# Second block's output projection: the groups' row scale ahead of the split, all partial sums in PSUM banks

## Chip, core and metric

One Trainium2 chip, one of its cores. The metric is the device time of one launch in microseconds (us); the kernel before is stated by the median of three runs.

## What is computed

Two blocks run one after the other on 256 tokens of width 1024, each two layers deep: a first block (latent attention, a gated recurrence, a gated feed-forward part) and a second block, a hybrid of windowed attention and a state-space mixer, with a gated feed-forward part. All inputs are float32. The part that matters is the end of the second block's mixer (`attn` has 512 columns, `y` 1024 in two groups of 512):

```
y = ssd_chunked(xs, dt, a_neg, bm, cm) + d_skip[:, None] * xs
y = y.reshape(bsz, s, SSM_INNER) * silu(z)
y = rmsnorm(y.reshape(bsz, s, 2, 512), ssm_norm.reshape(2, 512))     # a mean of squares per token and group
return concatenate([attn, y.reshape(bsz, s, 1024)], axis=-1) @ w_out   # 1536 x 1024, added to the residual x
```

Behind it comes `h = h + swiglu(rmsnorm(h))`, which needs the whole sum.

## The kernel before

Activations lie feature-major: a tile has 128 features on the partitions and the 256 tokens on the free axis; the residual stream `x` is eight such chunks. Products of float32 are made of three matmuls in fp32r (`mm3`, L434 to L436): each operand is split into a high and a low half, and high x high, high x low and low x high are accumulated in PSUM. Weights come by DMA in units of 128 x 1024 (`wf`), ScalarE copies the high half (`wh`, L409), VectorE subtracts to get the low half (`wl`, L410). There are three `wf` buffers and six each of `wh` and `wl`, used in turn, so the copy of a unit waits until TensorE is done with the unit six before it.

`layer_b` (L1021) is one layer of the second block. Its end: the gate `z` is multiplied out (L1255) and passed through silu; per pair p of chunks (0 to 3; group 0 is pairs 0 and 1, group 1 pairs 2 and 3) the state-space output is finished by matmuls (L1236, L1242) and VectorE's `dskip` step (L1238), product (L1244) and add (L1245). Then `out_residual` makes the attention part of the output projection: for each of four pairs of output chunks one unit of weights, 2 x 4 x 3 matmuls into a fresh PSUM bank (tag `mm`, four banks), and an add of the bank to `x` (L571). Each group is gated (L1264), squared (L1266), its squares added (L1273, L1275); its rows, scaled by the norm's gain alone, are split into high and low halves (L482, L483; tile `r`). `token_rsqrt` sums the squares over the partitions with a small matmul (L500), scales the mean (L502) and takes the power -1/2 on GpSimd (L503). `bcast_rows` spreads the result over the partitions: a diagonal tile `dg` (L489), a matmul with ones (L491), ScalarE's copy to `rb` (L493). `out_residual` runs again for each group on the unscaled rows: the bank is multiplied by `rb` on VectorE (L569), and added to `x` by GpSimd (L571), pair 3 of group 1 by VectorE. `ffn` follows: `norm_prep` splits `x` into `xs` (L482, L483), and `lin_wide` (L455, L456) multiplies.

Within an engine instructions run in one row; which row that is, a scheduler decides when the kernel is built, from its own plan of the engines, so instructions of several stages are interleaved.

## Time and profile before

| | us |
|---|---|
| median of three runs | 1431.85 (1431.1 to 1432.63) |
| the profiled execution | 1431.08 |
| its span, first to last instruction | 1429.3 |
| TensorE busy | 1410.8 |
| VectorE busy | 1125.7 |
| ScalarE busy | 853.9 |
| GpSimd busy | 137.0 |
| TensorE's mean granted clock | 0.995 |

The profiled execution is one run; its span leaves out 1.8 us around the first and last instruction. A busy TensorE is modelled from starts, since matmuls overlap: two matmuls of 256 columns start 0.12 us apart though each has a duration of 0.28. What counts is therefore where one starts against the one before it. In a timeline row a start, a duration, the engine, the source line and operation, the tiles (out<-in) and a count are followed in brackets by the idle time ahead of it and by what ended that.

### The profile page before, as it was taken

How to read it: one execution, taken by the hardware profiler on the slowest of the kernel's cores; microseconds unless marked ns; L12 is line 12 of the kernel's file. 1: busy time of each engine (PE TensorE's matmuls, PEld its weight loads, DVE VectorE, ACT ScalarE, POOL GpSimd, SP SyncE). 2: the span in 40 equal slices, each digit the busy share in tenths (PEclk: the TensorE clock that was granted, in tenths of full speed). 3: DMA queues.
4: the chain of work that ended last, by engine and by line, in shares of the span. 5: the costliest groups of instructions: out<-in, count | busy, mean ns of one | idle time of the engine just before them, and what ended most of it. 6: DMA issues, size and time to landing. Idle time of an engine off the chain costs nothing.

```text
span 1429.3 us, 25414 instructions
## 1 busy us (share of the span) xinstructions
PE 1410.8 (99%) x9668; PEld 1257.0 (88%) x9668; DVE 1125.7 (79%) x1907; ACT 853.9 (60%) x1517; POOL 137.0 (10%) x167
## 2 busy tenths in 40 slices
PE   9999999999999999999999998999999999999997
PEld 8888988888898889888888998988888998988886
DVE  7897778776678968887766989888766899988754
ACT  7666456654486655666546764566544784666543
POOL 4610000000033000000002010200000200400000
PEclk9999999999999999999999999999999999999999
DMA  7643556555565345556466653465556663465553
GB/s 246 200 145 122 177 163 199 193 166 181 183 208 176 119 133 178 177 193 199 146 195 214 193 178 105 155 196 181 166 185 195 194 192 113 146 202 190 176 174 106
DMA packets 86234, 248.64 MB, mean 174 GB/s; under 512 B 8992, under 2 KB 28768, under 8 KB 86112
## 3 DMA queue, kind: packets, MB, share of 16 engines
q1 hardware_dynamic: 85392, 246.11, 54.0%
q8 instruction: 76, 1.25, 0.3%
q10 hardware_dynamic: 720, 0.91, 0.2%
q14 instruction: 46, 0.38, 0.1%
HBM read 245.87 MB, written 1.11 MB: 173 GB/s over the span
## 4 chain that ended last, share of the span: by engine, by line
PE 76%; issue 14%; DVE 5%; DMA 2%; ACT 2%; POOL 1%; ACTq 0%; POOLq 0%; DVEq 0%
PE mm L455 26%; PE mm L456 13%; PE mm L435 7%; PE mm L434 7%; PE mm L436 7%; PE at L455 5%; PE at L456 3%; DVE wl L410 2%; DMA wf<-in_wa 2%; ACT wh L409 1%; PE at L606 1%; PE at L643 1%; PE at L632 1%; PE rc L900 1%; PE rc L606 0%
## 5 line engine op out<-in xcount | busy, mean ns | idle before, releaser
L410 DVE TENSOR_TENSOR wl<-wf,wh 128x1024 fp32r<-128x1024 f32 (+3 forms) x501 | 560.9, 1126 | 154.1 <-ACT wh L409 148.2
L409 ACT ACTIVATE wh<-wf 128x1024 fp32r<-128x1024 f32 (+3 forms) x501 | 485.2, 972 | 307.3 <-PE mm L455 110.6
L455 PE MATMUL mm<-xs,wh 128*128 128x512 f32 x1344 | 472.5, 394 | 0.0
L456 PE MATMUL mm<-xs,wl 128*128 128x256 f32 x1344 | 377.2, 282 | 0.0
L455 PEld LDWEIGHTS mm<-xs,wh 128*128 128x128 f32 x1344 | 251.3, 187 | 55.5 <-ACT q L778 0.4
L456 PEld LDWEIGHTS mm<-xs,wl 128*128 128x128 f32 x1344 | 253.6, 189 | 1.7 <-issue 0.2
L455 PE MATMUL at<-xs,wh 128*128 128x512 f32 x448 | 157.1, 392 | 0.0
L455 PE MATMUL mm<-h,wh 128*128 128x512 f32 x384 | 135.7, 395 | 0.5 <-DVE x L587 0.5
L456 PE MATMUL at<-xs,wl 128*128 128x256 f32 x448 | 125.2, 280 | 0.0
L456 PE MATMUL mm<-h,wl 128*128 128x256 f32 x384 | 107.0, 279 | 0.0
L503 POOL TENSOR_TENSOR ry<-ry,mhalf 128x2 f32<-128x2 f32 x13 | 13.5, 1038 | 960.1 <-DVE ry L502 881.5
L455 PEld LDWEIGHTS at<-xs,wh 128*128 128x128 f32 x448 | 83.9, 187 | 18.6
L435 PE MATMUL mm<-xs,wh 128*128 128x256 f32 x320 | 91.9, 287 | 0.0
L436 PE MATMUL mm<-xs,wl 128*128 128x256 f32 x320 | 91.3, 285 | 0.0
L434 PE MATMUL mm<-xs,wh 128*128 128x256 f32 x320 | 91.2, 285 | 0.0
L455 PE MATMUL mm<-t,wh 128*128 128x512 f32 x256 | 90.6, 394 | 0.0
L455 PEld LDWEIGHTS mm<-h,wh 128*128 128x128 f32 x384 | 72.0, 188 | 17.8 <-PE mm L456 1.1
L456 PEld LDWEIGHTS at<-xs,wl 128*128 128x128 f32 x448 | 84.5, 189 | 0.2
L672 ACT ACTIVATE pr<-mm 128x256 f32<-128x256 f32 x120 | 44.5, 375 | 61.1 <-PE mm L456 61.1
L587 DVE TENSOR_TENSOR x<-x,mm 128x256 f32<-128x256 f32 x96 | 39.1, 416 | 51.2 <-PE mm L456 51.1
L434 PE MATMUL mm<-r,wh 128*128 128x256 f32 x256 | 74.3, 293 | 4.7 <-DVE x L571 3.4
L435 PE MATMUL mm<-r,wh 128*128 128x256 f32 x256 | 74.9, 294 | 0.0
(339 smaller groups left out, 2713.1 us busy)
## 6 DMA issues: line engine op xcount, KB each, us to landing
wf<-in_fa SPq DMA_DIRECT2D x120, 512.0 KB, 4.0
wf<-in_fb SPq DMA_DIRECT2D x120, 512.0 KB, 4.0
wf<-in_wa SPq DMA_DIRECT2D x100, 512.0 KB, 4.1
wf<-in_wb SPq DMA_DIRECT2D x72, 512.0 KB, 3.9
wf<-in_fa SPq DMA_DIRECT2D x32, 192.0 KB, 2.4
wf<-in_fb SPq DMA_DIRECT2D x32, 192.0 KB, 2.4
r<-ad SPq DMA_DIRECT2D x16, 256.0 KB, 5.9
wf<-in_wa SPq DMA_DIRECT2D x8, 384.0 KB, 3.7
```

The costliest lines, as they stand in the source:

```text
L409: S.activation(wh[:, :c], f, AF.Copy)
L410: (G if self.i in self.pool else V).tensor_tensor(out=wl[:, :c], in0=f, in1=wh[:, :c].bitcast(F32), op=ALU.subtract)
L434: PE.matmul(ps, lhsT=sh, rhs=mh, start=start, stop=False)
L435: PE.matmul(ps, lhsT=sh, rhs=ml, start=False, stop=False)
L436: PE.matmul(ps, lhsT=sl, rhs=mh, start=False, stop=stop)
L455: PE.matmul(wide, lhsT=wh[:, j, c0:c0 + P], rhs=xs[k], start=k == 0, stop=False)
L456: PE.matmul(wide[:, 1], lhsT=wl[:, j, c0:c0 + P], rhs=xs[k][:, 0], start=False, stop=k == tot - 1)
L587: V.tensor_tensor(out=x[:, c], in0=x[:, c], in1=bank[:, o:o + T], op=ALU.add)
L606: PE.matmul(ps[:, h], lhsT=q, rhs=k[:, 0:n * P], start=True, stop=True)
L632: PE.transpose(pt[:, i], probs[u].rearrange("p h (a k) -> p (h a) k", k=P)[:, i], ident)
L643: PE.matmul(po[64 * j:64 * j + 64, i], lhsT=vs(a, 2 * c + j), rhs=PTs[2 * c + j][a], start=a == 0, stop=a == n - 1)
L672: S.activation(gu[:, m], bank[:, T:2 * T], AF.Copy)
```

## The change

The attention part and both groups go into the same accumulators: four banks `mm`, one for each pair of output chunks, except that the second chunk of pair 3 has a bank of its own with the tag `at`. No product is added to `x` in between; after group 1 each pair's bank is added once (pair 3 chunk by chunk). For that the row scale of a group can no longer be applied to the product: `scaled` computes the group's scale, multiplies rows by gain and scale on VectorE (`scalar_tensor_tensor`, eight a layer), and then splits them, in instructions of 512 columns. `gated` does gate, squares and sums earlier in the text. GpSimd has no residual add left, and the multiplications by `rb` are gone.

```diff
-    def lin_fm(ps, units, c0, xh, xl):
+    def lin_fm(ps, units, c0, xh, xl, first=True, last=True):
...
-                mm3(ps, wh[:, j, c0:c0 + P], wl[:, j, c0:c0 + P], xh[k], xl[k], k == 0, k == tot - 1)
+                mm3(ps, wh[:, j, c0:c0 + P], wl[:, j, c0:c0 + P], xh[k], xl[k],
+                    first and k == 0, last and k == tot - 1)
...
+        squares = []
+
+        def gated(g):
+            sq = []
+            for p in (2 * g, 2 * g + 1):
+                V.tensor_tensor(out=conv[p], in0=conv[p], in1=sz[g][:, p % 2], op=ALU.mult)
+                sq.append(sb("m", [P, 2, T]))
+                S.activation(sq[-1], conv[p], AF.Square)
+            V.tensor_tensor(out=sq[0], in0=sq[0], in1=sq[1], op=ALU.add)
+            a = sq[0][:, 0]
+            V.tensor_tensor(out=a, in0=a, in1=sq[0][:, 1], op=ALU.add)
+            squares.append(a)
+
+        def scaled(g):
+
+            rg = bcast_rows(token_rsqrt(squares[g], 1.0 / 512, EPS2), "rc")
+            yh, yl = [], []
+            for p in (2 * g, 2 * g + 1):
+                y = conv[p]
+                h2 = sb("r", [P, 2, T], F32R)
+                l2 = sb("r", [P, 2, T], F32R)
+                for m in range(2):
+                    V.scalar_tensor_tensor(out=y[:, m], in0=y[:, m], scalar=fm(f"ssmn{l}", 2 * p + m), in1=rg,
+                                           op0=ALU.mult, op1=ALU.mult)
+                split(h2, l2, y)
+                yh += [h2[:, m] for m in range(2)]
+                yl += [l2[:, m] for m in range(2)]
+            return yh, yl
...
+            if p == 1:
+                gated(0)
...
-        out_residual(st, mh, ml)
-        ys = []
-        for g in range(2):
...
-                    split(h2[:, m], l2[:, m], y[:, m], fm(f"ssmn{l}", 2 * p + m))
...
-            ys.append((yh, yl, bcast_rows(token_rsqrt(a, 1.0 / 512, EPS2), "at")))
-        for g in range(2):
-            out_residual(st, *ys[g], PA[g])
+        acc = [psm() for _ in range(4)]
+        acc_pair = [b.rearrange("p (m t) -> p m t", m=2) for b in acc]
+        acc = [b[:, m * T:m * T + T] for b in acc[:3] for m in range(2)] + [acc[3][:, 0:T], psq("at")[:, 0:T]]
+        for i in range(3):
+            hs, ls = scaled(i - 1) if i else (mh, ml)
+            for p in range(4):
+                u = st.next()
+                for m in range(2):
+                    c = 2 * p + m
+                    lin_fm(acc[c], u, m * P, hs, ls, i == 0 and (m == 0 or p == 3), i == 2 and (m == 1 or p == 3))
+                    if i == 2 and p == 3:
+                        V.tensor_tensor(out=x[:, c], in0=x[:, c], in1=acc[c], op=ALU.add)
+                if i == 2 and p < 3:
+                    ps = acc_pair[p]
+                    V.tensor_tensor(out=x[:, 2 * p:2 * p + 2], in0=x[:, 2 * p:2 * p + 2], in1=ps, op=ALU.add)
+            if i == 0:
+                gated(1)
```

How the engines' rows change is shown at three places of the first of the two layers; the second layer has the same there. In the changed kernel the line numbers of `mm3` are L433 to L435, those of the weight halves L408 and L409, of gate, add of squares and last add L1234, L1237 and L1239, of the scaling L1251.

TensorE, where the attention part ends (halves `sg` and `q`) and group 0 begins (halves `r`), before:

```order
L435 MATMUL mm_1743_9877<-q_1575_8784,wh_1740_9858 128x256
L436 MATMUL mm_1743_9877<-sg_1574_8783,wl_1741_9859 128x256
L434 MATMUL mm_1769_9963<-r_1745_9894,wh_1767_9958 128x256
L434 MATMUL mm_1774_9997<-r_1745_9894,wh_1772_9992 128x256
L434 MATMUL mm_1779_10031<-r_1745_9894,wh_1777_10026 128x256
L435 MATMUL mm_1769_9963<-r_1746_9895,wh_1767_9958 128x256
```

and changed:

```order
L434 MATMUL at_1733_9773<-q_1575_8784,wh_1744_9865 128x256
L435 MATMUL at_1733_9773<-sg_1574_8783,wl_1745_9866 128x256
L500 MATMUL rc_1748_9902<-ones_81,m_1713_9636 128x1 x2
L491 MATMUL rc_1751_9911<-dg_1750_9908,ones_81 128x256
L500 MATMUL rc_1769_10047<-ones_81,m_1746_9895 128x1 x2
L433 MATMUL mm_1729_9769<-r_1753_9915,wh_1758_9928 128x256
L433 MATMUL mm_1730_9770<-r_1753_9915,wh_1761_9958 128x256
```

The norms' small matmuls (group 0's L500 and L491, group 1's L500) now stand between the attention part and group 0; before they stood 60 and more matmuls further on, among the groups' own.

VectorE at the same place, changed (tile `m` holds the squares, `t` the rows, `dg` the diagonal, `rb` the spread scale):

```order
L409 TENSOR_TENSOR wl_1780_10074<-wf_1778_10072,wh_1779_10073 128x1024
L1239 TENSOR_TENSOR m_1713_9636<-m_1713_9636 128x256
L1225 TENSOR_TENSOR t_1643_9159<-t_1643_9159,hv_1696_9504 128x2x128
L1234 TENSOR_TENSOR t_1643_9159<-t_1643_9159,q_1698_9508 128x512
L409 TENSOR_TENSOR wl_1783_10105<-wf_1781_10103,wh_1782_10104 128x1024
L1234 TENSOR_TENSOR t_1643_9159<-t_1643_9159,q_1698_9508 128x512
L502 TENSOR_SCALAR ry_1749_9905<-rc_1748_9902 128x2
L1237 TENSOR_TENSOR m_1746_9895<-m_1746_9895,m_1747_9898 128x512
L489 TENSOR_SCALAR dg_1750_9908<-cst_78,ry_1749_9905 128x128 x2
L1239 TENSOR_TENSOR m_1746_9895<-m_1746_9895 128x256
L1251 SCALAR_TENSOR_TENSOR t_1611_8947<-t_1611_8947,pfm_76,rb_1752_9913 128x256 x4
L502 TENSOR_SCALAR ry_1770_10050<-rc_1769_10047 128x2
```

Between group 0's last add of squares (L1239) and its scaled mean (L502) stand two gates and a weight split; before, splits of the unscaled rows stood there, and the residual adds of the attention part ahead of them.

ScalarE around the end of group 0, before:

```order
L409 ACTIVATE wh_1819_10280<-wf_1818_10279 128x1024
L493 ACTIVATE rb_1754_9922<-at_1753_9920 128x256
L409 ACTIVATE wh_1822_10286<-wf_1821_10285 128x1024
L493 ACTIVATE rb_1765_9955<-at_1764_9953 128x256
L409 ACTIVATE wh_1830_10338<-wf_1829_10337 128x1024
```

and changed:

```order
L408 ACTIVATE wh_1785_10135<-wf_1784_10134 128x1024
L408 ACTIVATE wh_1788_10166<-wf_1787_10165 128x1024
L408 ACTIVATE wh_1799_10240<-wf_1798_10239 128x1024
L408 ACTIVATE wh_1802_10246<-wf_1801_10245 128x1024
L493 ACTIVATE rb_1773_10058<-rc_1772_10056 128x256
L482 ACTIVATE r_1774_10060<-t_1643_9159 128x512
L482 ACTIVATE r_1776_10066<-t_1643_9159 128x512
```

Group 1's spread scale and the splits of its rows now stand behind four weight copies, the last of which (`wh_1802`) takes the buffer of `wh_1767`, which group 0's last matmuls read.

## Rows read from the trace of the kernel before

**Rows 1.** The page, part 1: busy us (share of the span) xinstructions.

```profile
PE 1410.8 (99%) x9668; PEld 1257.0 (88%) x9668; DVE 1125.7 (79%) x1907; ACT 853.9 (60%) x1517; POOL 137.0 (10%) x167
```

**Rows 2.** Waits of TensorE in the whole span: us in total, times, longest us.

```profile
PE mm L434 <- DVE x L571: 3.4, 2, 1.7
PE rc L500 <- DVE m L1275: 1.6, 1, 1.6
PE mm L434 <- DVE ry L502: 1.2, 1, 1.2
```

**Rows 3.** Timeline of TensorE, first layer of the second block: start us, us.

```profile
871.47 0.28 PE L436 MATMUL mm<-sg,wl 128*128 128x256 f32 x1
...
875.60 0.28 PE L436 MATMUL mm<-sg,wl 128*128 128x256 f32 x1
875.72 0.28 PE L434 MATMUL mm<-r,wh 128*128 128x256 f32 x1
...
877.79 0.39 PE L434 MATMUL mm<-r,wh 128*128 128x256 f32 x1 [1.68 <-DVE x L571]
...
892.41 0.55 PE L434 MATMUL mm<-r,wh 128*128 128x256 f32 x1 [1.22 <-DVE ry L502]
...
908.52 0.40 PE L455 MATMUL mm<-xs,wh 128*128 128x512 f32 x1
```

**Rows 4.** Timeline of TensorE, second layer of the second block.

```profile
1206.47 0.40 PE L434 MATMUL mm<-r,wh 128*128 128x256 f32 x2
1208.55 0.38 PE L434 MATMUL mm<-r,wh 128*128 128x256 f32 x1 [1.68 <-DVE x L571]
...
1219.86 0.59 PE L491 MATMUL at<-dg,ones 128*128 128x256 f32 x2
...
1220.40 0.50 PE L500 MATMUL rc<-ones,m 128*128 128x1 f32 x4
...
1235.28 0.40 PE L455 MATMUL mm<-xs,wh 128*128 128x512 f32 x1
```

**Rows 5.** Windows: us, busy of PE, PEld, DVE, ACT, POOL; PEclk, DMA, GB/s.

```profile
891.62:898.45 6.83, 6.04 (x28) 6.07 (x29) 6.10 (x10) 1.06 (x1) 5.61 (x5) 0.50 0.45 144
1209.06:1212.48 3.42, 3.42 (x17) 3.42 (x18) 3.42 (x8) 0.00 (x0) 0.00 (x0) 0.50 0.11 43
```

**Rows 6.** Groups by line, GpSimd, 875.72 to 908.52: busy, mean ns | idle, releasers.

```profile
L571 POOL TENSOR_TENSOR x<-x,m 128x512 f32<-128x512 f32 (+1 forms) x8 | 10.3, 1300 | 10.5 <-DVE m L569 5.7 <-DVE ry L502 4.8
```

**Rows 7.** Timeline of VectorE, first layer.

```profile
868.05 1.66 DVE L1238 SCALAR_TENSOR_TENSOR t<-t,pfm,rc 128x256 f32<-128x256 f32 x4 [0.20 <-PE rc L1236]
...
871.03 1.22 DVE L410 TENSOR_TENSOR wl<-wf,wh 128x1024 fp32r<-128x1024 f32 x1
872.16 0.42 DVE L1244 TENSOR_TENSOR hv<-at,h 128x256 f32<-128x256 f32 x1
872.50 0.68 DVE L1264 TENSOR_TENSOR t<-t,q 128x512 f32<-128x512 f32 x1
...
877.66 0.87 DVE L483 SCALAR_TENSOR_TENSOR r<-t,pfm,r 128x256 fp32r<-128x256 f32 x2
```

**Rows 8.** Timeline of VectorE, a norm's scaled mean and diagonal, first and second layer.

```profile
885.66 0.16 DVE L502 TENSOR_SCALAR ry<-rc 128x2 f32<-128x2 f32 x1 [0.62 <-PE rc L500]
...
887.58 0.48 DVE L489 TENSOR_SCALAR dg<-cst,ry 128x128 f32<-128x128 f32 x2 [0.23 <-POOL ry L503]
...
1216.51 0.15 DVE L502 TENSOR_SCALAR ry<-rc 128x2 f32<-128x2 f32 x1
...
1217.93 0.48 DVE L489 TENSOR_SCALAR dg<-cst,ry 128x128 f32<-128x128 f32 x2 [0.60 <-POOL ry L503]
```

**Rows 9.** Timeline of ScalarE, first and second layer.

```profile
871.72 1.06 ACT L409 ACTIVATE wh<-wf 128x1024 fp32r<-128x1024 f32 x1 [0.98 <-PE mm L435]
...
873.21 0.63 ACT L1266 ACTIVATE m<-t 128x512 f32<-128x512 f32 x1 [0.43 <-DVE t L1264]
...
1220.49 0.39 ACT L493 ACTIVATE rb<-at 128x256 f32<-128x256 f32 x1 [1.29 <-PE at L491]
```

32 lines of the change are left out of this document (removed).

## The prediction

> **What bounds the kernel now.** I read the page's busy times first: TensorE is busy 99% of the span [rows 1], and the change leaves its count of matmuls as it is. So the time can move only by TensorE's idle time or its clock. The second view is the list of what TensorE waited for [rows 2]: 3.4 us in two waits for a residual add (L571: a PSUM bank that had not been emptied), 1.6 us for the sum of squares (L1275) and 1.2 us for the scaled mean (L502). All lie in the stage that the change rewrites.
>
> The third view is TensorE's own timeline of that stage. In the first of the two layers of the second block the attention part's last matmul starts at 875.60, the first matmul of the state-space groups at 875.72, and the feed-forward part at 908.52 [rows 3]: 32.80 us. In the second layer it is 1206.47 to 1235.28 [rows 4], 28.81 us. The groups' own work is 2 x 96 matmuls at 0.12 us a start (875.60 to 875.72 [rows 3]), 2 x 11.52 = 23.04 us. The rest is the waits above, the small matmuls of the two norms, and the clock: it was granted at 0.50 for 6.83 us and for 3.42 us there [rows 5]. So 9.8 and 5.8 us a layer is all that can be won.
>
> **The change, part by part.** Terms that hide. Per layer GpSimd loses its eight residual adds, 10.3 us [rows 6]; VectorE loses ten multiplications and, on balance, two adds and gains eight scalings; ScalarE's and VectorE's splits get half as many instructions, twice as wide. TensorE's matmuls cover all of that where nothing waits for it: 0. If the cover were gone it would be VectorE's net 3 us a layer, a gain. The wait for a PSUM bank (1.7 us a layer) goes, since the accumulators stay in their banks. The weights keep their order and their DMAs.
>
> The term that costs. Before, the groups were multiplied unscaled and the row scale was applied to the result, so the first matmul of group 0 needed nothing of the norm. Now the scale goes into the operand. In TensorE's new order the sum of squares of group 0, its broadcast, the sum of squares of group 1 and only then the first matmul of group 0 stand in a row, with no other matmul between. TensorE runs its row in order, so it idles until the whole chain is through. I follow the chain from 868.05, where VectorE takes up the `dskip` steps after waiting for TensorE's L1236 [rows 7]; up to there the two kernels have the same instructions, and from there VectorE has no gap.
>
> VectorE, first layer. When one instruction follows another at once it starts 0.08 before the row's end: 1.13 for a weight split (871.03 to 872.16), 0.34 for 256 columns (872.16 to 872.50), so 0.60 for 512 columns, 0.40 for each scaling step [rows 7]. Four `dskip` steps from 868.05 to 869.63; two adds 870.30; tile `hv` 870.64; gate 871.24; `hv` 871.58; gate 872.18; weight split 873.32; two `dskip` steps 874.11; add of squares 874.71; two `dskip` steps 875.50; add 875.84; weight split 876.98; last add of group 0's squares, 0.42, ends at 877.40. TensorE has been idle since 875.72.
>
> From there the chain has two strands. VectorE's own row goes on to 877.66 (add), 878.26 (gate), 879.40 (weight split), 880.00 (gate, ending at 880.08), and only then the scaled mean (L502) starts, at 880.00, although its matmul (0.50 [rows 4]) was through near 878.0. From its start to the diagonal tile's (L489), with GpSimd's power between, the trace has 1.92 and 1.42 us [rows 8]: 881.42 to 881.92. The other strand, ScalarE's square of the last pair (0.63 [rows 9]) and the add behind it, ends earlier, at 881.37. Diagonal 0.48 [rows 8], so 881.90 to 882.40; a handover between engines is 0.03 (872.50 + 0.68 to 873.21 [rows 7, 9]). The broadcast matmul to ScalarE's copy takes 0.63 (1219.86 to 1220.49 [rows 4, 9]), the copy 0.39 [rows 9], two scalings 0.87 (the row at 877.66 [rows 7]), ScalarE's split of 512 columns about 0.63 by the square of that width. Sum from the diagonal's end with handovers: 0.03 + 0.63 + 0.39 + 0.03 + 0.87 + 0.03 + 0.63 + 0.03 = 2.64. The first matmul of group 0 starts at 884.5 to 885.0; I take 884.8, **9.1 us** after 875.72.
>
> Group 1 has a second wait. Its mean and diagonal are early, but the broadcast matmul stands behind group 0's last matmul (start E), and on ScalarE the copy of the broadcast stands behind a weight copy (`wh`) that needs the buffer which that last matmul reads. A weight copy starts 0.25 after such a matmul (871.47 to 871.72 [rows 3, 9]) and takes 1.06, so E + 1.31; VectorE's weight split, which stands ahead of the scalings, E + 2.48; two scalings E + 3.35; split and two handovers E + 4.04. The next matmul would have started at E + 0.12: **3.9 us** idle. Behind the waiting instructions stand the feed-forward part's weights on both engines; they have the 11.5 us of group 1 to catch up, so that costs 0.
>
> Sum at full clock, a layer: 9.1 + 11.52 + 3.92 + 11.52 = 36.06 us against 32.80 and 28.81: +3.3 and +7.2, together **+10.5 us**. The old stage's waits and half-clock stretches are inside the times subtracted.
>
> The clock. After the stall that ended at 892.41 TensorE was at 0.50 until 898.45 [rows 3, 5]; after the one that ended at 1208.55, for 3.42 us until 1212.48 [rows 4, 5]; the first layer's stall that ended at 877.79 [rows 3] drew nothing. At 0.50 there were 17 matmuls in 3.42 us, 0.20 each [rows 5]. So a stall of 1.7 to 3 us cost 0, or 3.42 - 17 x 0.12 = 1.4, or 6.04 x (1 - 0.12/0.20) = 2.4 us. Four longer stalls are coming (9.1 and 3.9 us, twice); the nearest rows are the two that drew it, 1.9 on average: 4 x 1.9 = 7.6, ends 0 and 9.7. The Trainium skill (TensorE: Matmul & The Clock Gate, Terms) prices the lower level at half of the throttled time. By that it would be (3.0 + 1.7) / 2 x 4 = 9.4, an estimate from that page and these stretches, and 1.8 us more than my sum; the rows give 0.20 against 0.12, two fifths, and decide.
>
> Total 10.5 + 7.6 = 18.1. The profiled execution took 1431.08 (span 1429.3 plus 1.8 around it), which makes 1449.2; it lies 0.8 under the median of 1431.85, so as a median I say 1449.7, slower by 1.2%.
>
> **The rivals.** (a) The clock stays at full, or is back at once: 1431.85 + 10.5 = 1442.4. For it: the stall at 877.79. Against: the new stalls are twice to five times as long.
> (b) Only one of the two stalls shows, because group 1's copy of the broadcast isn't held behind the weight copy: 2 x (3.9 + 1.9) less, 1438.1. Against it: the order on ScalarE is a fixed row.
> (c) The other side: group 0's chain is through in the shadow of the attention matmuls, TensorE never idles, and the stage takes 23.04 us plus some 1.5 for the norms' small matmuls (L491 0.59, L500 0.50 [rows 4], twice). Then 8.3 and 4.3 us are won: 1419.3. It decides at the end of the last add of group 0's squares: the first matmul follows 7.4 us behind that (877.40 to 884.8), so for no idle time it has to end by 868.3. That is when VectorE only begins group 0's `dskip` steps at the earliest, held by TensorE itself [rows 7]. That speaks strongly against it.
> (d) The feed-forward part's first matmuls find the banks still full, as at 877.79 and 1208.55: 2 x 1.7 more, 1453.1. The Trainium skill (Trainium Kernel Development and Optimization, Best Practices) says that steady bubbles can mean PSUM has run out; the two waits for L571 agree with it for the old kernel [rows 2]. In the new order the first two banks that are needed belong to the pairs done first, with 48 and more matmuls behind them, so I give it little.
>
> **How the numbers follow.** Forecast (stalls and clock) 0.70, (a) 0.15, (b) 0.05, (c) 0.04, (d) 0.06. The forecast's own ends: chain 0.3 either way a layer and the clock at 1.4 to 2.4 a stall, 1447.3 to 1452.3. The range takes in (a) and (d) with such a margin: 1441 to 1455, 0.91 of the chance, leaving out (b) and (c). This kernel's measurement can tell about 0.2% from no change, 2.9 us. Faster by more than that 0.04; within it 0.01, since no case ends there; slower 0.95.
>
> **What would show it.** In the new profile: TensorE idle for about 9 us between the last attention matmul and the first of group 0, released by ScalarE's split of the scaled rows, and for about 4 us ahead of group 1, in both layers; VectorE without a gap from 868 to 880; the granted clock at 0.50 behind each stall; no more GpSimd adds and no wait for a residual add. Wrong would be a first matmul of group 0 before 882, TensorE taking group 0 up ahead of the norm's matmuls, or a feed-forward part that starts under 35 us after the attention part ended.

## The result, and the profile after

The changed kernel takes **1450.23 us** (median of four runs, 1448.74 to 1450.93) against 1431.75 us on the same chip: ratio 1.012, 95% interval 1.0107 to 1.0133. It is slower by 18.5 us; 1449.7 was predicted. Its profiled execution took 1448.74, with a span of 1446.95.

The page's first part of the changed kernel (columns as in [rows 1]), and the waits of TensorE in the whole span (columns as in [rows 2]):

```profile
PE 1414.7 (98%) x9668; PEld 1262.5 (87%) x9668; DVE 1109.1 (77%) x1891; ACT 852.4 (59%) x1509; POOL 111.3 (8%) x151
```

```profile
PE mm L433 <- ACT r L482: 9.4, 4, 3.3
PE rc L491 <- DVE dg L489: 7.9, 2, 3.9
PE rc L500 <- DVE m L1239: 3.3, 2, 1.6
```

GpSimd and VectorE have less to do than before (26 and 17 us less), and TensorE the same 9668 matmuls in 18 us more. Where [rows 2] had two waits for a full bank (3.4 us, L571), there is none. In their place stand 20.6 us in eight waits, and each of them belongs to the norm: the last add of squares (L1239), the diagonal tile (L489), the high half of the scaled rows (L482). TensorE's timeline of the first layer's stage shows where they lie; it answers to [rows 3]:

```profile
875.37 0.28 PE L435 MATMUL at<-sg,wl 128*128 128x256 f32 x1
877.27 0.58 PE L500 MATMUL rc<-ones,m 128*128 128x1 f32 x4 [1.63 <-DVE m L1239]
881.79 1.19 PE L491 MATMUL rc<-dg,ones 128*128 128x256 f32 x2 [3.94 <-DVE dg L489]
882.77 0.85 PE L500 MATMUL rc<-ones,m 128*128 128x1 f32 x4
885.03 0.80 PE L433 MATMUL mm<-r,wh 128*128 128x256 f32 x2 [1.41 <-ACT r L482]
...
898.35 0.28 PE L435 MATMUL at<-r,wl 128*128 128x256 f32 x1
898.47 0.59 PE L491 MATMUL rc<-dg,ones 128*128 128x256 f32 x2
902.37 0.87 PE L433 MATMUL mm<-r,wh 128*128 128x256 f32 x4 [3.31 <-ACT r L482]
...
915.48 0.40 PE L455 MATMUL mm<-xs,wh 128*128 128x512 f32 x1
```

Attention's last matmul starts at 875.37, the first of group 0 at 885.03 and not at 875.49: 9.54 us idle of large matmuls, in which TensorE runs only the ten small ones of the norms. After group 0's last, at 898.35, there is a second hole up to 902.37. The stage, from attention's last matmul to the feed-forward part's first, takes 40.11 us here and 40.65 in the second layer; before it was 875.60 to 908.52, 32.92, and 28.93. Together +18.9 us: the loss lies in the stage that was rewritten. VectorE shows what the first hole is made of; this timeline answers to [rows 7, 8]:

```profile
876.71 0.42 DVE L1239 TENSOR_TENSOR m<-m 128x256 f32<-128x256 f32 x1
877.04 0.42 DVE L1225 TENSOR_TENSOR t<-t,hv 128x256 f32<-128x256 f32 x1
877.38 0.69 DVE L1234 TENSOR_TENSOR t<-t,q 128x512 f32<-128x512 f32 x1
877.98 1.22 DVE L409 TENSOR_TENSOR wl<-wf,wh 128x1024 fp32r<-128x1024 f32 x1
879.11 0.69 DVE L1234 TENSOR_TENSOR t<-t,q 128x512 f32<-128x512 f32 x1
879.72 0.15 DVE L502 TENSOR_SCALAR ry<-rc 128x2 f32<-128x2 f32 x1
880.56 0.69 DVE L1237 TENSOR_TENSOR m<-m,m 128x512 f32<-128x512 f32 x1 [0.69 <-ACT m L1236]
881.16 0.48 DVE L489 TENSOR_SCALAR dg<-cst,ry 128x128 f32<-128x128 f32 x2
...
883.44 1.67 DVE L1251 SCALAR_TENSOR_TENSOR t<-t,pfm,rb 128x256 f32<-128x256 f32 x4 [1.46 <-ACT rb L493]
```

The sums of squares are through TensorE before 878, yet the scaled mean (L502) starts at 879.72, since an add, a gate, a weight split and a second gate, none of them needed for it, stand ahead of it in VectorE's row. The second hole begins on TensorE's own row, where group 1's broadcast (L491) stands behind group 0's last matmul, and grows on ScalarE, whose timeline answers to [rows 9]:

```profile
898.55 1.06 ACT L408 ACTIVATE wh<-wf 128x1024 fp32r<-128x1024 f32 x1 [1.34 <-PE at L434]
899.51 0.37 ACT L493 ACTIVATE rb<-rc 128x256 f32<-128x256 f32 x1
901.69 0.63 ACT L482 ACTIVATE r<-t 128x512 fp32r<-128x512 f32 x1 [1.81 <-DVE t L1251]
```

Group 1's copy of the broadcast starts 0.96 us behind a weight copy that had waited for TensorE's last readers of its buffer, and ScalarE then waits for VectorE's scaling, ahead of which a weight split stands. By the prediction's own steps (0.63 from the broadcast to the copy, then 0.39, 0.87, 0.63 and three handovers of 0.03) the next large matmul could have followed the broadcast's start at 898.47 by 2.6 us, at 901.1; it came at 902.37. So, as an estimate from these rows, 1.3 of the 3.9 us belong to the weight copy and the split, and 2.6 to the broadcast's place on TensorE's row. The windows in which the clock was granted at 0.50 (columns as in [rows 5]), and two neighbouring matmuls in the first of them:

```profile
878.94:889.18 10.24, 5.98 (x25) 5.75 (x26) 5.78 (x16) 2.27 (x4) 1.80 (x2) 0.50 0.21 82
902.83:906.24 3.41, 3.41 (x18) 3.41 (x17) 0.91 (x2) 0.29 (x1) 0.00 (x0) 0.50 0.29 102
1216.86:1227.10 10.24, 6.92 (x30) 6.69 (x31) 4.85 (x13) 2.27 (x4) 1.72 (x2) 0.50 0.16 52
1240.75:1244.16 3.41, 3.41 (x18) 3.41 (x18) 0.48 (x1) 0.00 (x0) 0.00 (x0) 0.50 0.15 60
```

```profile
886.27 0.41 PE L434 MATMUL mm<-r,wh 128*128 128x256 f32 x1
886.48 0.41 PE L435 MATMUL mm<-r,wl 128*128 128x256 f32 x1
```

All four holes drew it. The first of a layer drew it already while TensorE stood idle (from 878.94), the second 0.46 and 0.98 us after work had resumed. In the windows matmuls start 0.213 us apart (from 886.27 to 888.83, twelve times), against 0.12 at full clock, so 0.44 of such time is lost.

### The profile page after: what moved, and what is told of

Its sections match the earlier page's. It is cut to its first block, busy times and chain, and to the rows that moved or that the text cites. A ratio compares the mean times of both kernels' runs of the same rounds, so it can differ in the third digit from the quotient of the medians.

```text
span 1447.0 us, 25348 instructions
## 1 busy us (share of the span) xinstructions
PE 1414.7 (98%) x9668; PEld 1262.5 (87%) x9668; DVE 1109.1 (77%) x1891; ACT 852.4 (59%) x1509; POOL 111.3 (8%) x151
## 4 chain that ended last, share of the span: by engine, by line
PE 78%; issue 13%; DVE 4%; ACT 2%; DMA 1%; POOL 1%; ACTq 0%; POOLq 0%; DVEq 0%
PE mm L455 27%; PE mm L456 14%; PE mm L433 8%; PE mm L434 8%; PE mm L435 8%; PE at L455 5%; PE at L456 3%; DVE wl L409 1%; PE at L586 1%; ACT wh L408 1%; PE at L623 1%; DMA wf<-in_wa 1%; PE rc L880 1%; PE at L612 1%; DVE t L1218 0%
## 5 line engine op out<-in xcount | busy, mean ns | idle before, releaser
L409 DVE TENSOR_TENSOR wl<-wf,wh 128x1024 fp32r<-128x1024 f32 (+3 forms) x501 | 557.4, 1120 | 172.7 <-ACT wh L408 167.8
L408 ACT ACTIVATE wh<-wf 128x1024 fp32r<-128x1024 f32 (+3 forms) x501 | 485.6, 973 | 337.5 <-PE mm L455 131.1
L435 PE MATMUL mm<-xs,wl 128*128 128x256 f32 x320 | 91.3, 285 | 0.0
L433 PE MATMUL mm<-xs,wh 128*128 128x256 f32 x320 | 91.2, 285 | 0.0
L433 PE MATMUL mm<-r,wh 128*128 128x256 f32 x240 | 69.6, 301 | 9.4 <-ACT r L482 9.4
L456 PEld LDWEIGHTS mm<-h,wl 128*128 128x128 f32 x384 | 72.3, 188 | 0.2
```

Of the source, the lines that this page charges most:

```text
L408: S.activation(wh[:, :c], f, AF.Copy)
L409: (G if self.i in self.pool else V).tensor_tensor(out=wl[:, :c], in0=f, in1=wh[:, :c].bitcast(F32), op=ALU.subtract)
L433: PE.matmul(ps, lhsT=sh, rhs=mh, start=start, stop=False)
L435: PE.matmul(ps, lhsT=sl, rhs=mh, start=False, stop=stop)
L456: PE.matmul(wide[:, 1], lhsT=wl[:, j, c0:c0 + P], rhs=xs[k][:, 0], start=False, stop=k == tot - 1)
```

## The experiments

Ratios are to the kernel before. Stage means, as above, attention's last matmul to the feed-forward part's first, first and second layer, in the profiled execution. Whole spans shift against each other by up to 4 us within their first 80 us, long before this stage; so I also compare the *rest*, from the start of TensorE's 4600th matmul (counting from 0; about 640 us) to the span's end: 788.85 us before, 806.73 after. Inserted lines move line numbers by two in some kernels: L491, L493, L504 and L505 are then the diagonal, the broadcast matmul, the scaled mean and the power, L435 to L437 `mm3`.

### Is it the norm's chain?

```diff
-            rg = bcast_rows(token_rsqrt(squares[g], 1.0 / 512, EPS2), "rc")
+            rg = rb
```

> What is left out: both groups' norms. `scaled` multiplies the rows by the layer's own spread scale `rb`, which is there long before, in place of the group's mean, power and spread; all else, the accumulators, the scaling ahead of the split, the one residual add a pair, is as in the changed kernel. Theory (the norm's chain, put on TensorE's row ahead of group 0, is what costs): in the changed kernel the first matmul of group 0 starts 9.5 us after the attention part and the first of group 1 3.7 us after group 0's end. Without the chain VectorE still has to scale and split group 0's rows: counted in its own order from 868.05 the first low halves are there near 879.2, so some 3 us of idle time are left ahead of group 0 and none ahead of group 1. The stage falls from 40.0 and 40.5 us to about 27 (23.04 of matmuls, 3 of idle time, 1 to 2 of half clock): 1424 us, 1419 to 1428. Rival (holding the four banks, or a later feed-forward part, is what costs): the banks are held as long as before, so at most the half clock goes: 1440 or more.

Measured 1424.94 us, ratio 0.9938 (0.9924 to 0.9953); stage 27.68 and 26.20, rest 781.23, 25.5 less than with the norm. So the accumulation costs nothing by itself; with the norm's chain gone the new arrangement is faster than the old one by 7.6 us of the rest. Not all of that is its own gain: this kernel leaves out the norms' small matmuls too (24 in the trace), which among large ones take some 0.37 us for a sum (885.00 to 885.48 in the kernel before, less one start) and 0.24 for a broadcast, 2.4 us in all. What is left of TensorE's waits there, and the one window at 0.50:

```profile
PE mm L434 <- DVE r L483: 5.6, 2, 2.8
```

```profile
882.52:885.93 3.41, 3.41 (x19) 3.41 (x18) 3.25 (x6) 0.72 (x2) 0.00 (x0) 0.50 0.73 246
```

The two equal waits, for the low half of group 0's rows, drew the lower clock in the first layer and not in the second. In all else the two stages run alike, and the first is 1.48 us longer: that is what 3.41 us at half clock cost, 0.43 of them.

### The second hole alone

```diff
-            hs, ls = scaled(i - 1) if i else (mh, ml)
+            hs, ls = ahead if i == 2 else scaled(0) if i else (mh, ml)
             for p in range(4):
+                if i == 1 and p == 2:
+                    ahead = scaled(1)
```

> Computes the same. `scaled(1)` stands ahead of group 0's third pair in the text, so that group 1's broadcast matmul stands in the middle of group 0's matmuls on TensorE's row and its copy ahead of the last weight copies on ScalarE's. Theory (the second stall is ScalarE's copy of the spread scale queued behind the weight copy that waits for group 0's last matmul): the idle time of 3.6 us beyond a start ahead of group 1 and the half clock that follows it (3.41 us, of which some 1.4 is lost) go in both layers: 2 x (3.6 + 1.4) = 10.0 less than 1450.2, so 1440 us, 1438.5 to 1442. The wait for ScalarE's L482 falls from four times to two. Rival (it is VectorE's four scalings and the weight splits around them that are late, whatever the order of the copy): the stall stays at 2 us or more, 1445 to 1450. Second rival (the stall moves to where the broadcast now stands): an idle time of 1 us or more in the middle of group 0, 1443 to 1448.

Measured 1441.99 us, ratio 1.0059 (1.0043 to 1.0075); stage 35.13 and 36.03, rest 797.53: 9.2 us less than the change. The wait for the scaled high half falls from four times to two, and the waits of the first hole stay as they were (3.2 us for the last add of squares):

```profile
PE rc L491 <- DVE dg L489: 7.9, 2, 3.9
PE mm L433 <- ACT r L482: 2.8, 2, 1.4
```

The second hole, with its window at 0.50, is worth 4.6 us a layer by the rest. The prediction had 5.8: 3.9 of idle time and 1.9 of clock. The idle time is gone, and the clock behind it cost 1.5 (3.41 us at the 0.44 above); some of that came back among group 0's matmuls, where the broadcast now takes 0.24 us.

Which of the two causes went shows on TensorE, ScalarE and VectorE:

```profile
897.13 0.59 PE L491 MATMUL rc<-dg,ones 128*128 128x256 f32 x2
```

```profile
897.21 1.06 ACT L408 ACTIVATE wh<-wf 128x1024 fp32r<-128x1024 f32 x1 [0.98 <-PE mm L434]
898.17 0.37 ACT L493 ACTIVATE rb<-rc 128x256 f32<-128x256 f32 x1
```

```profile
899.44 1.67 DVE L1251 SCALAR_TENSOR_TENSOR t<-t,pfm,rb 128x256 f32<-128x256 f32 x4
```

The copy still stands behind a weight copy, and starts 1.04 us after the broadcast as it did in the change; the scaling starts 2.31 after it, where it was 2.30. So the hole went because the chain now lies under matmuls of group 0, and not because the queue on ScalarE got shorter. No run took the weight copy alone out of the way.

### The clock alone

The kernel above with 60 matmuls a layer that nothing reads (12, 32 and 16), between the steps of the first hole.

```diff
+                def idle(n):
+                    for _ in range(n):
+                        spare = tc.keep_in_program_order(PE.matmul(scratch[:, 0:T], lhsT=u[0][0][:, 0, 0:P], rhs=mh[0], start=True, stop=True))
+                    return spare
...
+                idle(12)
...
+                spare = idle(16)
```

> Computes the same, with work added that nothing reads: as e2_g1_early (group 1's chain early, so only the first stall is left), and in the first stall 60 matmuls of 256 columns into a spare bank, 12 ahead of the sum of squares, 32 ahead of the broadcast and 16 behind it, 0.12 us each, in both layers. They fill 7.2 of the 9.5 us and are there to hold the clock. Theory (the stall costs twice: its length, and the half clock after it): the clock stays at full through the stage, the stall keeps its length to within 0.5 us (the small float32 matmuls of the norm get faster: 0.3 in place of 0.56 for a half of the broadcast). After e2_g1_early's stalls the clock was at 0.50 for 3.45 and 5.51 us; two fifths of that are 1.4 and 2.2, and 0.4 a layer for the small ones: 4.4 less than e2_g1_early, whose time from TensorE's 4600th matmul to the span's end was 797.53: 793.1, and 1437.5 us, 1436 to 1439.5. Rival (the half clock costs nothing, since other engines limit group 0's start): the same as e2_g1_early, 797 to 798. Second rival (the added matmuls delay the chain): the stall grows by 1 us or more, 798 or more.

Measured 1436.6 us, ratio 1.0021 (1.0012 to 1.003); stage 32.91 in both layers, 2.2 and 3.1 us less than without the filler. The longest run of fillers starts at 878.41 and lasts 4.08 us (32 matmuls). The window of its first stage:

```profile
875.40:910.00 34.60, 34.26 (x278) 33.63 (x278) 26.30 (x47) 17.21 (x26) 1.80 (x2) 1.00 0.42 136
```

The clock stays at 1.00, and the way from attention's last matmul to group 0's first falls from 9.66 to 8.96 us, because the chain's own matmuls run at full clock too. So the lower clock of the first holes costs 5.3 us, over both layers. The rest falls by 2.2 only, as 3.1 us came up in the second layer's attention, where there is a wait (1.6 us, L629) and a window of 3.41 us at 0.50 behind it (1.5 us).

### Scaling ahead of the split, without accumulating

Each product has a bank of its own again and is added to `x`; the scaling stays ahead of the split.

```diff
-                    lin_fm(acc[c], u, m * P, hs, ls, i == 0 and (m == 0 or p == 3), i == 2 and (m == 1 or p == 3))
...
+                    ps = psm()[:, 0:w * T].rearrange("p (m t) -> p m t", m=w)
+                    for m in range(w):
+                        lin_fm(ps[:, m], u, (n + m) * P, hs, ls)
+                    c = 2 * p + n
+                    V.tensor_tensor(out=x[:, c:c + w], in0=x[:, c:c + w], in1=ps, op=ALU.add)
```

> Computes the same; one part of the change alone. The groups are scaled ahead of their split, as in the changed kernel, but nothing is kept in the banks: each of the twelve products has a bank of its own and is added to the residual by VectorE, as it was for the attention part. Theory (the scaling ahead of the split costs, the accumulating gains): the norm's chain stands on TensorE's row as before this run, and VectorE's row in front of the scaled mean is longer by the attention part's five residual adds (some 2.2 us of them beyond what fell away) and, ahead of group 1's scaling, by three of group 0's (1.5 us). Stalls of 11.5 and 5.3 us in place of 9.5 and 3.7, with the same half clock: 2 x 3.7 more than 1450.2, 1457.5 us, 1453 to 1461. Rival (accumulating in four held banks is what costs): the stage is near that of the kernel before, 1428 to 1440. Second rival (the residual adds are hidden): 1449 to 1452.

Measured 1456.76 us, ratio 1.0161 (1.0148 to 1.0175); stage 42.10 and 43.02, rest 812.04, 5.3 more than the change. Its longest wait:

```profile
PE rc L500 <- DVE m L1239: 10.2, 2, 5.1
```

On VectorE the adds of the attention products (0.68 us each) stand ahead of the last add of squares, which now ends at 884.64, and that wait grows from 1.6 to 5.1 us a layer. The wait for the diagonal behind it falls from 3.9 to 2.1, so that the first hole is longer by 2.0 us. The second hole stays as it was, where 5.3 us were expected. The two halves of the change pull in opposite directions: without the accumulation the two stages are 4.4 us longer, while the scaling ahead of the split alone leaves the rest 23.2 us above the kernel before. (The other 0.9 of the 5.3 us came up in the first layer's feed-forward part, whose matmuls ran at the slower of two spacings told of at the end.)

### Can the first hole be shortened by taking work out of VectorE's row?

First by giving two of VectorE's weight splits of this stretch to GpSimd:

```diff
-    WL_POOL = ()
+    WL_POOL = (20, 21)
```

> Computes the same. Two of the weight splits (the low halves of group 0's third and fourth unit) go from VectorE to GpSimd, in both layers. Theory (the first stall is as long as VectorE's row is from 868.05 on, and the row between the last add of group 0's squares and the scaled mean belongs to it): 2 x 1.13 us of that row go, one of the two gates also falls behind the scaled mean, so L502 starts near 876.9 in place of 879.72 and the first matmul of group 0 near 882.5 in place of 885.03: 2.5 us a layer, 1445 us, 1443 to 1447. Rival (the stall is set by TensorE's own sum of squares, by GpSimd's power or by ScalarE's split): first matmul of group 0 within 0.5 us of 885, 1449 to 1451. Second rival (GpSimd's subtraction slows VectorE's beside it, or the power waits behind it): the gain is under 1 us a layer, or a loss, 1449 to 1455.

Measured 1450.45 us, ratio 1.0114 (1.0099 to 1.0129); stage 39.81 and 40.78, rest 806.38: nothing gained, where 5 us were expected. VectorE's and GpSimd's timelines:

```profile
873.45 2.53 DVE L1234 TENSOR_TENSOR t<-t,q 128x512 f32<-128x512 f32 x1
```

```profile
872.71 2.72 POOL L409 TENSOR_TENSOR wl<-wf,wh 128x1024 fp32r<-128x1024 f32 x1 [1.78 <-ACT wh L408]
881.05 2.24 POOL L503 TENSOR_TENSOR ry<-ry,mhalf 128x2 f32<-128x2 f32 x1 [5.62 <-DVE ry L502]
```

The gate, 0.68 alone, took 2.53 us beside GpSimd's split, and the power, 0.73 in the changed kernel, took 2.24 beside a weight split of VectorE. That is 3.4 us more, where the move had freed 2 x 1.14 us in VectorE's row.

Then by the order: group 1's gates and the later weight splits behind group 0's chain, over the early `scaled(1)` from above.

```diff
+            if i == 1:
+                chain = dict(last)
+                with tc.issue_after(chain["low"]):
+                    gated(1)
...
+                with tc.issue_after(chain["low"]) if i == 1 and p >= 2 else ExitStack():
+                    u = st.next()
```

> Computes the same, in another order within the rows of two engines. On VectorE the two gates of group 1 (with its squares and adds) and the weight splits of group 0's third and fourth unit are queued behind the low split of group 0's rows; on TensorE the pairs of each group follow one another. GpSimd gets nothing, so the slowing that E3 ran into is out of the way. Theory (the first stall is the time that VectorE's row needs from the `dskip` steps to the diagonal tile, work of others in it included): without three weight splits and two gates the last add of squares ends before the attention part does, so the sum of squares follows at once, L502 starts near 876.1 in place of 879.72 (in the clock of the changed kernel's trace), the broadcast matmul near 877.8 in place of 881.79, and the first matmul of group 0, 3.24 behind it, near 881.1 in place of 885.03: 5.6 us idle in place of 9.5. The second stall stays at 3.7 to 4.2. So 4.0 us a layer, 8.0 together: 1442 us, 1440 to 1444; from one and the same instruction ahead of the stage (TensorE's 4600th matmul) to the end of the span 798.7 in place of 806.73. Rival (the stall is set by other engines' handovers, E3's result): first matmul within 1 us of 885, 1448 or more.

Measured 1450.33 us, ratio 1.0119 (1.0103 to 1.0134); stage 39.99 and 39.97, rest 806.08. The first hole did shrink, to 5.01 us between matmuls (877.18 to 882.19; 9.66 in the change). But the total stayed, against an expected 1442. VectorE and TensorE at the second hole:

```profile
900.85 1.22 DVE L409 TENSOR_TENSOR wl<-wf,wh 128x1024 fp32r<-128x1024 f32 x1 [2.90 <-ACT wh L408]
901.99 1.27 DVE L1253 SCALAR_TENSOR_TENSOR t<-t,pfm,rb 128x256 f32<-128x256 f32 x3
```

```profile
903.58 0.58 PE L435 MATMUL mm<-r,wh 128*128 128x256 f32 x1 [6.36 <-ACT r L484]
```

The deferred splits ended up ahead of group 1's scaling and wait for weight copies there; the second hole grew to 6.4 us in the first layer and 5.2 in the second, from 3.3 of the same wait.

Last, the chain of group 1 is put inside group 0's matmuls and pinned there, over the order just shown.

```diff
+                ahead = scaled(1)
+                g1 = dict(last)
...
-                with tc.issue_after(chain["low"]) if i == 1 and p >= 2 else ExitStack():
+                with tc.issue_after(g1["low"] if i == 2 else g1["diag"] if p == 3 else chain["low"]) if i == 2 or i == 1 and p >= 2 else ExitStack():
...
-                    with tc.issue_after(last["mm"]) if i else ExitStack():
+                    with tc.issue_after(g1["spread"] if i == 1 and p == 2 and m == 0 else last["mm"]) if i else ExitStack():
```

> Computes the same; the changed kernel with the best order that was found for it. As e4_chain_first, and group 1's chain is brought through inside group 0: its gates and squares follow group 0's low split on VectorE, its broadcast stands ahead of group 0's third pair on TensorE, and the weight splits of the fourth pair and of group 1 are queued behind its diagonal tile and its low split. Theory (in e4_chain_first the 4.65 us won ahead of group 0 came back ahead of group 1, because the deferred gates, squares and weight splits were then in front of group 1's scaling): with those behind, the first stall stays at 5.0 us and the second goes, but for some 0.8 ahead of group 0's third pair. One half-clock stretch a layer is left, some 2 us lost in it. Stage 5.0 + 23.04 + 1.2 + 0.8 + 2 = 32 us in both layers; from TensorE's 4600th matmul to the span's end 806.73 - (40.11 - 32) - (40.65 - 32) = 790.0, against 788.85 in the kernel before: 1433 us, 1430 to 1436, about the kernel before and no better. Rival (the work comes back once more, ahead of the feed-forward part or in its beginning): stage under 34, but 1438 or more. Second rival (the first stall can go entirely by order): stage 27 or less, 1425 or less.

Measured 1434.5 us against 1434.03, ratio 1.0002 (0.9993 to 1.0011); stage 31.81 and 32.51, rest 789.99 (790.0 expected). What is left in TensorE's waits:

```profile
PE rc L493 <- DVE dg L491: 4.4, 4, 1.7
PE mm L435 <- ACT r L484: 4.1, 2, 2.1
```

That is group 0's chain at its shortest here: 5 us a layer in which no large matmul can run. Against the kernel without the norms the two stages are 10.4 us longer, which eats up the 8.0 us by which that kernel's stages were shorter than before: the best order that I found for the change is level with the kernel before.

### A kernel that keeps one half

If only group 0's chain can't be hidden, group 0 alone can stay as it was: attention and group 1 accumulate; group 0 goes unscaled into banks of its own and is multiplied by its scale afterwards, while its matmuls cover group 1's chain.

```diff
+        hs, ls = raw(0)
+        rg = bcast_rows(token_rsqrt(squares[0], 1.0 / 512, EPS2), "rc")
...
+            ps = psq("at").rearrange("p (m t) -> p m t", m=2)
...
+                behind(order, lambda: lin_fm(ps[:, m], u, m * P, hs, ls))
+            y = sb("m", [P, 2, T])
+            g0[f"mult{p}"] = behind(g1["low"] if p == 3 else None, lambda: V.tensor_tensor(out=y, in0=ps, in1=rows(rg, 2), op=ALU.mult)).ins
+            G.tensor_tensor(out=x[:, 2 * p:2 * p + 2], in0=x[:, 2 * p:2 * p + 2], in1=y, op=ALU.add)
```

> Computes the same, by a middle way. Attention and group 1 accumulate in the four banks; group 0 keeps the old way, unscaled rows into banks of their own (two, tag `at`), multiplied by the spread scale afterwards and added by GpSimd. So group 0's 96 matmuls stand between the attention part and the first matmul that needs a norm. The small matmuls of the norms, the pairs' order and the weight splits of group 1 are pinned in the rows. Theory (the stall is the length of a norm's chain that no matmul covers; 11.5 us of matmuls cover it): group 0 starts with the attention part's end, group 1's chain is through by the end of group 0, no idle time over 1 us in the stage. Stage 23.04 + 1.5 of small matmuls + at most 1.5 = 25 to 26 us, against 40.0 and 40.5: 1421 us, 1417 to 1427, under the kernel before too (1431.75). Rival (holding the four banks through the stage is what costs): stage 35 us or more, 1440 or more. Second rival (the old way's bank wait of 1.7 us a layer comes back, longer, since group 0 has two banks): 1427 to 1434.

Measured 1432.13 us, ratio 0.9997 (0.9985 to 1.001); stage 27.72 and 28.04, rest 784.82. Where 1421 us were expected, the time is level with the kernel before. The long holes are gone, but waits of 0.6 us (diagonal) and 0.3 us (low half) stay, and in the second layer's feed-forward part matmuls came more slowly: 455 in 80 us here, 464 in the changed kernel, both at clock 1.00:

```profile
1260.00:1340.00 80.00, 80.00 (x455) 69.37 (x454) 65.33 (x107) 50.96 (x92) 0.00 (x0) 1.00 0.58 186
```

```profile
1284.00:1364.00 80.00, 80.00 (x464) 70.53 (x463) 65.88 (x109) 50.65 (x92) 0.00 (x0) 1.00 0.59 190
```

To see whether that was chance, the same kernel ran again, with no edit.

> The kernel of e6_mixed once more, word for word, with another profile. In its first profile the stage was shorter than in the kernel before by 5.2 and 0.9 us (27.72 and 28.04 in place of 32.92 and 28.93), but the last feed-forward part, whose instructions are the same, was longer by 2.5 us: a pair of its matmuls took 350 ns in place of 347. Theory (that pitch is a matter of the execution, not of the kernel): in another profile the last feed-forward part has a pitch of 347 and takes 194.0 to 194.4 us from its first matmul to the span's end, and the time from TensorE's 4600th matmul to the end is 782.3 in place of 784.8 (788.85 in the kernel before). Rival (the new order brings the slower pitch on, by where it lets the part begin): 196.5 and 784.8 again. Either way the time is 1425 to 1433, and the ratio to the kernel before 0.995 to 1.000.

Measured 1431.13 us, ratio 0.9984 (0.9974 to 0.9994); stage 27.71 and 28.01, rest 787.61. The slower pitch came again, now in parts of both layers' feed-forward parts. The rests of these two executions of one kernel differ by 2.8 us, some 2.0 of it by the pitch, so a difference of that size between single profiles need not be the kernels' doing. What sets the pitch I can't say.

Next GpSimd's adds were held behind the power of group 1's norm, and a weight split behind its diagonal.

```diff
-            G.tensor_tensor(out=x[:, 2 * p:2 * p + 2], in0=x[:, 2 * p:2 * p + 2], in1=y, op=ALU.add)
+            behind(g1["pow"], lambda: G.tensor_tensor(out=x[:, 2 * p:2 * p + 2], in0=x[:, 2 * p:2 * p + 2], in1=y, op=ALU.add))
...
-            u = behind((g0["mult1"], g1["low"], g1["low"], g1["low"])[p], st.next)
+            u = behind((g1["diag"], g1["low"], g1["low"], g1["low"])[p], st.next)
```

> Computes the same. The middle way of e6_mixed with two more pins: GpSimd's adds of group 0 to the residual are queued behind group 1's power, and VectorE's split of group 1's first weights behind group 1's diagonal tile. Theory (in e6_mixed group 1's diagonal tile took 1.51 us in place of 0.48 and its scaling 2.17 in place of 1.67, beside GpSimd's adds, so that TensorE waited 0.85, 0.57 and 0.73 us for group 1's chain): the diagonal tile takes 0.5 and those three waits fall under 0.3 us each; the stage goes from 27.7 and 28.0 to 26.0 to 26.5, the time from TensorE's 4600th matmul to the span's end from 784.8 (first profile) or 787.6 (second profile) to 782 to 785; 1427 to 1430 us, 0.994 to 0.998 of the kernel before. Rival (GpSimd's adds only move on to slow the scaling and the splits behind it): the diagonal tile is short, the waits for the low splits (0.57 and 0.73) stay or grow, stage 27 to 28.5.

Measured 1437.5 us, ratio 1.0026 (1.0016 to 1.0037); stage 31.60 and 31.51, longer by 3.9 and 3.5 us, with 3.41 us at half clock in each layer again. VectorE, and GpSimd at the same time:

```profile
886.84 2.54 DVE L491 TENSOR_SCALAR dg<-cst,ry 128x128 f32<-128x128 f32 x2 [0.21 <-POOL ry L505]
...
891.04 2.70 DVE L1253 SCALAR_TENSOR_TENSOR t<-t,pfm,rb 128x256 f32<-128x256 f32 x4
```

```profile
886.77 2.53 POOL L1312 TENSOR_TENSOR x<-x,m 128x512 f32<-128x512 f32 x2
```

The adds now fell right upon the chain's diagonal (0.48 alone) and its scaling (1.67 alone). So they were moved out of the chain, behind group 1's low halves.

```diff
+        late = G.tensor_tensor(out=gate, in0=ls[3][:, 0:2].bitcast(F32), in1=mhalf[:, 0:1].to_broadcast([P, 2]), op=ALU.mult).ins
+        for p in range(4):
+            behind(late, lambda: G.tensor_tensor(out=x[:, 2 * p:2 * p + 2], in0=x[:, 2 * p:2 * p + 2], in1=products[p], op=ALU.add))
```

> Computes the same. The middle way once more, with GpSimd's four adds of group 0's products to the residual kept out of group 1's chain altogether: the products of the first two pairs are left in the tiles of group 0's rows, which are free by then, and the adds are queued on GpSimd behind a tiny operation that reads the low half of group 1's rows. VectorE's split of group 1's first weights stands behind group 1's diagonal tile. Theory (in e6_mixed and e10_mixed_tuned the diagonal tile of group 1 took 1.51 and 2.54 us in place of 0.48, its four scalings 2.17 and 2.70 in place of 1.67, because GpSimd's adds ran beside them): the diagonal tile takes 0.48 and the scalings 1.67 again, group 1's chain is through 2 us earlier, TensorE's waits for it (2.2 us a layer in e6_mixed) fall under 0.7, and the stage goes from 27.7 and 28.0 to 25.5 to 26.3. From TensorE's 4600th matmul to the span's end 781 to 782 where the feed-forward parts run at 173.3 ns a matmul, up to 786 where they run at 176.7; 0.992 to 0.997 of the kernel before. Rival (the diagonal tile and the scalings are slow for another reason): they take 1.5 and 2.2 us as before, stage 27.5 to 28. Second rival (the late adds slow group 1's weight splits instead): TensorE waits 1 us or more for a weight split in group 1 or in the feed-forward part, stage 27 or more.

Measured 1430.73 us, ratio 0.9987 (0.9976 to 0.9998); stage 26.06 and 26.11 as expected, but the ratio isn't (0.992 to 0.997 was), and the rest is 785.81. VectorE in that stage:

```profile
887.58 0.48 DVE L491 TENSOR_SCALAR dg<-cst,ry 128x128 f32<-128x128 f32 x2 [0.81 <-POOL ry L505]
...
890.17 1.67 DVE L1253 SCALAR_TENSOR_TENSOR t<-t,pfm,rb 128x256 f32<-128x256 f32 x4 [0.16 <-ACT rb L495]
...
893.75 6.55 DVE L409 TENSOR_TENSOR wl<-wf,wh 128x1024 fp32r<-128x1024 f32 x3
```

The chain has its old durations again, the stage is the shortest of all, but three weight splits beside the adds take 6.55 us instead of 3.4, and the feed-forward part then waits 1.3 us a layer (L655). Whether the one comes of the other is not shown. Last, VectorE makes the adds itself.

```diff
-            behind(late, lambda: G.tensor_tensor(out=x[:, 2 * p:2 * p + 2], in0=x[:, 2 * p:2 * p + 2], in1=products[p], op=ALU.add))
+            behind(g1["low"], lambda: V.tensor_tensor(out=x[:, 2 * p:2 * p + 2], in0=x[:, 2 * p:2 * p + 2], in1=products[p], op=ALU.add))
```

> The same as the kernel before it (attention and group 1 accumulate, group 0 multiplied by its scale afterwards), but the four adds of group 0's products to x are made by VectorE, one ahead of each of group 1's weight splits, so that GpSimd does nothing there. In that kernel the three weight splits beside GpSimd's adds took 6.55 us (3.4 alone), and the feed-forward part then waited 1.3 us a layer for VectorE. Theory (working side by side costs more than the adds themselves): the weight splits are back at 1.13 us each, the four adds take 2.4 us, so VectorE is through 0.7 us earlier, and the wait in the feed-forward part falls below 0.8 us; stage 25.5 to 26.3 us in both layers; from TensorE's 4600th matmul to the end 783 us (781 to 785.5), against 785.8; ratio to the kernel before the change 0.9965 (0.994 to 0.9985). Rival (the wait in the feed-forward part has nothing to do with GpSimd, since its own norm ends last): the splits are short again but the wait stays at 1.3, and the time is that of the other kernel, ratio 0.9985 to 0.9995. Another: the four adds on VectorE now stand ahead of weight splits that TensorE waits for, and group 1 stalls by 0.6 us a pair: ratio 1.000 to 1.002.

Measured 1429.28 us against 1433.24, ratio **0.9972** (0.9959 to 0.9986); stage 27.81 and 27.17, rest 785.07. The first of VectorE's three weight splits, and TensorE's waits in the feed-forward part:

```profile
893.51 1.22 DVE L409 TENSOR_TENSOR wl<-wf,wh 128x1024 fp32r<-128x1024 f32 x1
```

```profile
PE mm L457 <- DVE xs L485: 3.0, 2, 1.8
PE at L457 <- DVE pr L655: 1.6, 1, 1.6
```

The splits are back at 1.22. But part of the gain went into a wait at another place: the first split of the feed-forward part's input (`xs`) now stands behind a weight split, 1.8 and 1.2 us; the wait at L655 is gone in the first layer and not in the second. This is the one kernel with the norms whose gain on the kernel before, 0.28%, is over the 0.2% that the prediction took for the least that can be told from no change. The second run of the first mixed kernel (0.16%) and the kernel with late adds (0.13%) lie under that, though their intervals too end short of 1. Against the rest of the kernel ahead of it (785.81) that is 0.7 us, so how much of the step in the ratio belongs to the adds is open.

## Why the prediction was right

**The bound** (TensorE, so only its idle time and its clock count): right. VectorE lost 17 us of work and GpSimd 26, and the kernel got slower.

**The hidden terms** at 0: nearly. No wait for a bank is left, and none names GpSimd. But between the holes the groups took 0.10 to 0.23 us more than 11.52 and their share of half clock, 0.54 us over the four (worked out from the matmul starts in both layers). That was not in the sum.

**Group 0's chain**: right in every step up to the diagonal. Attention ends 0.23 us earlier in the new trace; shifted by that, the predicted end of the last add is 877.17 (877.13 measured), the scaled mean 879.77 (879.72), the diagonal from 881.19 (881.16). That is the early end of the stretch it was given; the forecast went by its middle, 0.28 later. The last term was mis-sized: from the diagonal's end, 881.64, to the first matmul it took 3.39 us instead of 2.64. Of the 0.75 more, 0.6 is the broadcast matmul: it ran at half clock, 881.79 to ScalarE's copy at 883.02, 1.23 instead of 0.63. The prediction put the lower clock behind the hole only; it came inside it. The two errors, 0.75 and 0.28, partly cancel: idle time 9.54 us instead of 9.1.

**Group 1's second wait**: the size right, the weight of its causes not. The next matmul was forecast at 4.04 us after group 0's last, and came at 4.02, by the steps named. But the prediction made ScalarE's weight copy the cause that decides, and by the estimate above that copy and VectorE's split are worth 1.3 of the 3.9 us, the broadcast's place on TensorE's row 2.6. The run that moved the broadcast took the hole away with the weight copy still ahead of group 1's copy.

**The clock**: the mechanism was right, the size a little high, by two errors that go against each other. The 0.20 us a matmul was 17 matmuls divided into a window [rows 5]; the starts themselves lie 0.213 apart, in the old kernel's window from 1209.06 too, so 0.44 of such time is lost and not two fifths. And at half clock after the holes lie 4.15, 3.41, 5.08 and 3.41 us, together 16.05, where the forecast took four times 4.73. That makes 7.0 us, against 7.6. The Trainium skill (TensorE: Matmul & The Clock Gate, Terms), by which half of such time is lost, would make it 8.0, an estimate from that page; two runs here lie nearer to the starts. The kernel without the norms shows 1.48 us for a window of 3.41, where one half would be 1.7. The filler experiment gave 5.3 us for the first holes: 0.44 of the 3.45 and 5.51 us that the kernel without filler worked at half clock behind them, with 1.2 for the two broadcasts, is 5.1, and one half makes 5.7.

**The sum**: the stage came out 0.8 over the forecast (+18.9 against +18.1), as +0.85 of idle time, +0.54 of small waits and -0.6 of clock. The whole gained 1.0 back in the first layer's feed-forward part, whose second part ran at 149 matmuls in 26 us before (1047 to 1073) and at 151 now (1054 to 1080). That spacing was in no term of the prediction, so a part of how closely the median was met is luck, errors that cancelled. The last step has a slip as well: 1431.85 and 18.1 make 1449.95, not 1449.7, and the low end of the forecast 1447.1.

**The rivals**: (a) full clock fell with the four windows at 0.50; the filler shows what it would have been worth. (b) fell: both holes show. Its price was too high besides: it took the whole second hole for the copy's place behind the weight copy, which by the same estimate is worth, with the split, 1.3 us of it. (d) fell: no wait for a bank. (c) is the interesting one. Its condition, a chain that ends before 868.3, was far off, and no order of the change that I ran came nearer than a 5 us hole. Its price was not reached either: without the norms, and so without their small matmuls, the same arrangement gives 1424.94 against 1432.45, 7.5 us less where (c) had 12.6. Of that the best kernel with the norms, in which group 0 doesn't wait for its chain, kept 4.0 (1429.28 against 1433.24).

## What to carry to other kernels

A scale that moves from a product to an operand moves its whole chain of reductions ahead of the first matmul: count that chain, from the last step that makes its input to the operand's halves, against the matmuls that are left to cover it, before counting what the accumulation saves. Split such a change: here the operand whose chain other matmuls cover (group 1) gains a little by it, and the one whose chain is exposed (group 0) must not wait. And work that is taken out of one hole or given to another engine must be followed to where it comes back.

## What the runs showed of the hardware that was not expected

Some instructions of VectorE and GpSimd held one another up when both engines were at work: a gate 2.53 us instead of 0.68, a diagonal tile 2.54 instead of 0.48, four scalings 2.70 instead of 1.67, three weight splits 6.55 instead of 3.4, a power of two columns 2.24 instead of 0.73. The Trainium skill (SBUF — State Buffer, section on SBUF's two separate sides) tells of a pair of ports that the two engines share under an exclusive lock, for VectorE's instructions with two inputs in SBUF among others. The gate agrees: it began 0.74 us after GpSimd's split (872.71 to 875.43), and ended 0.55 us behind it, at 875.98, which is little less than the 0.68 that it takes alone. Not every pair is held up: in the kernel with GpSimd's adds behind the power, that power (886.11, 0.70 us) ran beside a multiplication by `rb` (885.94, 0.68), and both kept their times.

The feed-forward matmuls run at one of two spacings over long stretches, 173.3 or 176.7 ns (mean over 96 starts), at full clock and with no wait in between: 464 or 455 in 80 us, worth some 2 us over the first part of a layer's feed-forward stage and 1 over the second. The kernel before had the slow one in the first layer's second part, the changed kernel in neither layer, and the kernel that ran twice in different parts each time. No run shows what chooses; it took back a part of what the mixed kernels gained.

Equal holes didn't draw equal clocks: without the norm a wait of 2.8 us drew 3.41 us at half clock in one layer and none in the other, as the two 1.68 us waits of [rows 3, 4] had done.
